# Reordering the opening of a two-layer attention decoder: the norm ahead of the modulation, sums in PSUM, four first weights instead of five

## The chip, the cores and the metric

The kernel runs on one core of a Trainium2 chip. The metric is the device time of one execution in microseconds, and the number used is the median over runs. The core has five engines with an instruction queue each, which run in order and wait for one another through semaphores: TensorE (PE, matmuls; its weight loads are listed as PEld), VectorE (DVE), ScalarE (ACT), GpSimd (POOL) and SyncE (SP), which here issues nearly all DMAs. SBUF is the working memory; PSUM is the memory that matmuls write, used here in eight banks of 128 x 512 float32.

## What is computed

Two layers of a decoder over 1024 tokens of width 1024. In each layer the input x is normalised (RMS over the width), scaled and shifted by a modulation that comes from a conditioning vector c, projected, mixed by two kinds of attention, gated, projected back and added to x. The change concerns only the start of the first layer:

```
cond  = silu(c)
mod   = cond @ w_ada[0] + b_ada[0]            # 3 x 1024: shift, scale, gate
h     = rmsnorm(x, g_pre[0]) * (1 + scale) + shift
z     = h @ ev_w_in[0]                         # the products
z_cq, z_ckv, z_kr, ... = split(z)              # first 384 columns, next 256, ...
q     = rmsnorm(z_cq, q_norm) @ w_uq           # and so on, unchanged
```

## The kernel before

Everything is kept transposed: width on the 128 partitions, tokens along the free axis, in two halves of C = 512 tokens, chunk 0 and chunk 1. So x is 2 x 8 tiles of 128 x 512, and a column block of z for one chunk is a sum over eight `kc` (128 rows of the width each). To keep float32 accuracy each h tile and each weight tile is split into a high and a low part, and each (weight block, kc) takes three matmuls (L127, L128, L130, in `kstep`): weight high by h high, weight high by h low, weight low by h high. A weight block of 128 columns thus takes 24 matmuls of 128x512 for a chunk.

The opening is written out by the string `PLAN`, whose letters the loop in `run` takes one after the other:

- `x`, `y`: issue the loads of chunk 0 or chunk 1 of x (eight DMAs of 256 KB on SP's queue).
- `r`, `s`: the norm of chunk 0 or 1. `squares` squares the eight tiles on ScalarE and adds them on VectorE (L194); `rstd` adds over partitions with a PE pass against ones (L204), computes the reciprocal square root by a chain of eleven small VectorE operations of 128 x 4 (L206 to L212), and spreads it back over 512 columns with matmuls against the identity (L216, "the transposes" below) into PSUM. `copied` moves that row block r to SBUF on ScalarE (L366).
- `A`: one of four groups of the modulation (two shift tiles and two scale tiles, so what two kc of h need). `ada` loads eight raw tiles of `w_ada`, multiplies each by its value of cond and adds them up (the first on ScalarE, L285; the other seven on VectorE, L282) into an SBUF tile `acc`; `mod_tiles` adds over partitions with a PE pass against ones (L294) and finishes the values with small VectorE operations (L303, L305).
- `W`: load a weight block, split it (high on ScalarE L91, low on GpSimd L92), and give it a PSUM bank. The blocks are the three of z_cq and the first of z_ckv, and before the change also the second.
- `n`, `m`: make the h tiles of chunk 0 or 1 that can be made (`pre_norm`): x times scale times r on VectorE (L325), plus shift on ScalarE as the high part (L331), and the low part by a subtraction on VectorE (L332). For odd kc, with `spread`, ScalarE does two operations and GpSimd does the subtraction.
- `P`: the products of all weight blocks at hand with the h tiles made since.

After the plan the opened weight blocks are evacuated, multiplied with chunk 1, and evacuated again; `keep` (L671 to L678) does this for z_cq and z_ckv and, after the last block of each, runs `rstd` for their norms. Then `project` goes on with the remaining blocks, through the same PSUM banks.

The string is the order in which the program is written. The tile library then orders each engine's instructions by priority, in which `high_priority` moves some ahead, and inserts the waits; the order shown below is that of the built program. Tiles with one tag share a fixed number of buffers (`bufs`), and a load into a buffer waits until the last reader of its former content is done. PSUM has the tags S (one tile of two banks), pt, pj and o (two banks each).

## Time and profile before

| | us |
|---|---|
| median of three runs | 1384.69 (1383.99 to 1385.03) |
| the profiled execution | 1385.66 |
| its span, first to last instruction | 1383.9 |
| its mean granted TensorE clock | 0.984 of full speed |
| TensorE busy | 1281.1 (93% of the span) |
| VectorE busy | 918.0 (66%) |
| ScalarE busy | 731.9 (53%) |
| GpSimd busy | 334.2 (24%) |

In the rows of the profile L12 is line 12 of the kernel, `out<-in` are the program's names without buffer numbers, and a row in order of time gives start and duration in us, engine, line, operation, shapes and count; the bracket behind it tells how long the engine had been idle and what released it. Matmuls are pipelined, so the distance between the starts of two of them says more than the duration of one. The span is 1.8 us shorter than the execution's time.

### The profile page before, as it was taken

The numbers are of one execution on the slowest core, as the hardware profiler recorded it, in microseconds if no ns is written. First come the engines' busy times: TensorE is split into PE (matmuls) and PEld (weight loads), VectorE is DVE, ScalarE is ACT, GpSimd is POOL, SyncE is SP. The second block draws the span as 40 slices with busy tenths as digits, with TensorE's granted clock in tenths as the row PEclk, the third lists the DMA queues.
The fourth block names the chain that finished last, engine by engine and source line by source line (L and its number), as shares of the span: only waits on it lengthen the run. The fifth ranks groups of instructions, "written<-read, shape, count | busy, mean of one in ns | idle before, by whom it ended". The sixth has DMA issues, their size and how long they took to land.

```text
span 1383.9 us, 20791 instructions
## 1 busy us (share of the span) xinstructions
PE 1281.1 (93%) x6940; PEld 1060.0 (77%) x6940; DVE 918.0 (66%) x1963; ACT 731.9 (53%) x1507; POOL 334.2 (24%) x316
## 2 busy tenths in 40 slices
PE   2798999999999999899989999999999999999996
PEld 2577788888777777777767778787888888888896
DVE  6855666777668775787977785767645464655375
ACT  4252126665557577764545544446445454556552
POOL 2242422331233215300013232221212111112400
PEclk9899999999999999999999999999999999999998
DMA  8605586556354544373633222212112121233283
GB/s 291 236 19 168 169 286 221 164 168 178 97 172 132 158 132 131 108 232 110 193 89 94 75 70 68 57 49 88 58 46 75 49 85 54 84 107 107 77 262 127
DMA packets 105132, 175.98 MB, mean 127 GB/s; under 512 B 16688, under 2 KB 25904, under 8 KB 105024
## 3 DMA queue, kind: packets, MB, share of 16 engines
q1 hardware_dynamic: 100512, 172.03, 39.4%
q10 hardware_dynamic: 4512, 2.62, 0.6%
q8 instruction: 54, 0.88, 0.3%
q14 instruction: 54, 0.44, 0.1%
HBM read 131.45 MB, written 31.74 MB: 118 GB/s over the span
## 4 chain that ended last, share of the span: by engine, by line
PE 59%; DVE 21%; issue 7%; ACT 6%; DMA 5%; POOL 1%; SPq 1%; DVEq 0%; POOLq 0%; ACTq 0%
PE pj L127 10%; PE pj L128 10%; PE pj L130 9%; PE S L441 7%; PE pt L500 4%; PE o L510 2%; DVE p L463 2%; PE S L127 2%; PE S L130 2%; PE o L509 2%; PE S L128 2%; DVE pt_l L92 2%; PE pt L216 1%; DVE acc L282 1%; DMA wr<-in_wout_dram 1%
## 5 line engine op out<-in xcount | busy, mean ns | idle before, releaser
L127 PE MATMUL pj<-h,wh 128*128 128x512 f32 (+1 forms) x816 | 340.6, 418 | 1.0 <-ACT wh L91 1.0
L128 PE MATMUL pj<-h,wh 128*128 128x512 f32 (+1 forms) x816 | 321.6, 394 | 0.0
L130 PE MATMUL pj<-h,wl 128*128 128x512 f32 (+1 forms) x800 | 314.9, 394 | 2.7 <-DVE wl L92 2.7
L92 POOL TENSOR_TENSOR wl<-wr,wh 128x512 fp32r<-128x512 f32 x126 | 164.2, 1311 | 462.7 <-ACT wh L91 424.4
L465 ACT ACTIVATE p<-p,sm 128x128 f32<-128x128 f32 (+3 forms) x192 | 148.7, 775 | 148.0 <-DVE sm L463 143.5
L92 DVE TENSOR_TENSOR pt_l<-pt,pt_h 128x512 fp32r<-128x512 f32 (+1 forms) x232 | 147.1, 635 | 107.4 <-ACT pt_h L91 105.7
L441 PE MATMUL S<-qk,qk 96*128 96x512 f32 (+5 forms) x720 | 174.6, 344 | 20.4 <-DVE sm L463 10.9
L91 ACT ACTIVATE pt_h<-pt 128x512 fp32r<-128x512 f32 (+1 forms) x232 | 127.8, 552 | 96.1 <-PE pt L500 92.5
L130 PEld LDWEIGHTS pj<-h,wl 128*128 128x128 f32 x800 | 150.5, 188 | 34.5 <-DVE wl L92 3.6
L441 PEld LDWEIGHTS S<-qk,qk 128*128 128x128 f32 (+1 forms) x720 | 120.8, 189 | 62.6 <-DVE sm L463 26.2
L127 PEld LDWEIGHTS pj<-h,wh 128*128 128x128 f32 (+1 forms) x816 | 153.6, 188 | 19.0 <-ACT wh L91 1.9
L128 PEld LDWEIGHTS pj<-h,wh 128*128 128x128 f32 (+1 forms) x816 | 154.1, 189 | 16.3 <-DVE h L92 0.2
L91 ACT ACTIVATE wh<-wr 128x512 fp32r<-128x512 f32 x165 | 101.2, 622 | 111.2 <-PE S L128 40.8
L500 PE MATMUL pt<-ident,p 128*128 128x128 f32 x840 | 134.4, 274 | 2.6 <-DVE p L944 2.6
L500 PEld LDWEIGHTS pt<-ident,p 128*128 128x128 f32 x840 | 101.2, 140 | 25.6 <-DVE p L944 4.1
L463 DVE CUSTOM_DVE_ANT_0 p<-S,mask 128x640 f32<-128x640 f32 (+7 forms) x128 | 95.9, 749 | 32.7 <-PE S L441 32.1
L509 PE MATMUL o<-pt_h,v 128*128 128x256 f32 (+1 forms) x408 | 106.5, 281 | 1.3 <-ACT pt_h L91 0.8
L510 PE MATMUL o<-pt_l,v 128*128 128x256 f32 (+1 forms) x408 | 102.3, 285 | 4.9 <-DVE pt_l L92 4.7
L347 POOL TENSOR_TENSOR t<-t,rs 128x512 f32<-128x512 f32 x26 | 36.8, 1417 | 230.8 <-DMA t<-t 208.3
L510 PEld LDWEIGHTS o<-pt_l,v 128*128 128x128 f32 x408 | 77.2, 189 | 14.8 <-DVE pt_l L92 9.6
L509 PEld LDWEIGHTS o<-pt_h,v 128*128 128x128 f32 x408 | 77.1, 189 | 9.5 <-ACT pt_h L91 3.4
L463 DVE CUSTOM_DVE_ANT_0 p<-S,x 128x128 f32<-128x128 f32 (+3 forms) x64 | 48.2, 753 | 25.0 <-PE S L445 21.8
(315 smaller groups left out, 2311.3 us busy)
## 6 DMA issues: line engine op xcount, KB each, us to landing
wr<-in_wod_dram SPq DMA_DIRECT2D x80, 256.0 KB
wr<-in_wout_dram SPq DMA_DIRECT2D x68, 256.0 KB
ad<-in_wadab_dram SPq DMA_DIRECT2D x41, 256.0 KB
wr<-in_wev_dram SPq DMA_DIRECT2D x38, 256.0 KB
raw<-in_wadaa_dram SPq DMA_DIRECT2D x32, 256.0 KB
ogd<-t SPq DMA_DIRECT2D x32, 256.0 KB
t<-t SPq DMA_DIRECT2D x106, 64.0 KB
t<-rd SPq DMA_DIRECT2D x48, 128.0 KB
```

The costliest lines, as they stand in the source:

```text
L91: nc.scalar.activation(hi, src, AF.Copy)
L92: (lo_eng or nc.vector).tensor_tensor(out=lo, in0=src, in1=hi.bitcast(F32), op=ALU.subtract)
L127: nc.tensor.matmul(p, w[0][:, k, :m], h[0], start=first, stop=False)
L128: nc.tensor.matmul(p, w[0][:, k, :m], h[1], start=False, stop=last and w[1] is None)
L130: nc.tensor.matmul(p, w[1][:, k, :m], h[0], start=False, stop=last)
L347: nc.gpsimd.tensor_tensor(out=s, in0=s, in1=self.rs[:, cs], op=ALU.mult)
L441: nc.tensor.matmul(dst, a, k[:, s], start=(n == 0), stop=(n == len(q) - 1 and not more))
L463: nc.vector.tensor_tensor_reduce(out=P[:, :n], in0=S[:, :n], in1=add, scale=-scale, scalar=init, op0=ALU.add, op1=ALU.min, accum_out=nm)
L465: nc.scalar.activation(P[:, :n], P[:, :n], AF.Exp, bias=nm, scale=-1.0, accum_out=l)
L500: nc.tensor.transpose(pt[:, n * 128:n * 128 + 128], b, self.ident)
L509: nc.tensor.matmul(o[:, qcols], w, hi[:, cols], start=start, stop=False)
L510: nc.tensor.matmul(o[:, qcols], w, lo[:, cols], start=False, stop=stop)
```

## The change

The plan is a new string. The norm of chunk 0 (`r`) comes before the first group of the modulation, each group's h tiles and products (`n`, `P`) stand ahead of the next group, the loads of chunk 1 (`y`) come after the second group, and its norm (`s`) at the end. There are four `W` instead of five, so the second block of z_ckv is done later by `project`. The sums of squares and the sums of the modulation are now kept in PSUM, in banks of the tags pt and o, until the last addition, which goes to SBUF because PE reads it. The row block r stays in PSUM (in a bank of pj for chunk 0, pt for chunk 1) and is no longer copied. The odd h tiles of chunk 0 are made like the even ones (`spread` is False). There are 12 raw buffers instead of 10. Line numbers behind `squares` shift by one.

```
--- before.py
+++ after.py
@@ -28,7 +28,7 @@
 
 
 
-PLAN = "xAWWrnWyPAWnAPWnsAPnnmmmmP"
+PLAN = "xrAWWnWPAnPyAWnPAsnPmmmmP"
 
 
 class Trunk:
@@ -185,16 +185,15 @@
     def squares(self, tiles):
 
         nc = self.nc
+        acc = self.psum("pt")
         for i, t in enumerate(tiles):
-            s = self.tmp()
+            s = self.tmp() if i else acc
             nc.scalar.activation(s, t, AF.Square)
-            if i == 0:
-                acc = s
-            else:
-                nc.vector.tensor_tensor(out=acc, in0=acc, in1=s, op=ALU.add)
-        return acc
-
-    def rstd(self, s, n, col=None):
+            if i:
+                nc.vector.tensor_tensor(out=acc if i < len(tiles) - 1 else s, in0=acc, in1=s, op=ALU.add)
+        return s
+
+    def rstd(self, s, n, col=None, home="pt"):
 
 
         nc = self.nc
@@ -211,7 +210,7 @@
             z = col if i == 2 and col is not None else y
             nc.vector.scalar_tensor_tensor(out=z, in0=w, scalar=1.5, in1=y, op0=ALU.add, op1=ALU.mult)
         y = z
-        r = self.psum("pt")[:, :nb * 128]
+        r = self.psum(home)[:, :nb * 128]
         for b in range(nb):
             nc.tensor.matmul(r[:, b * 128:b * 128 + 128], y[:, b:b + 1].to_broadcast([128, 128]), self.ident,
                              start=True, stop=True)
@@ -270,19 +269,21 @@
         nc.sync.dma_start(self.rc, I["rc"])
         nc.sync.dma_start(self.rs, I["rs"])
 
-    def ada(self, l, w, tiles, a, raw):
+    def ada(self, l, w, tiles, a, raw, part=None):
+
 
         nc = self.nc
         n = 128 * len(tiles)
         a = a[:, :n]
+        part = a if part is None else part[:, :n]
         for kc in range(8):
             r = raw()[:, :n]
             nc.sync.dma_start(r, w(kc))
             if kc:
-                nc.vector.scalar_tensor_tensor(out=a, in0=r, scalar=self.sc[:, kc:kc + 1], in1=a,
+                nc.vector.scalar_tensor_tensor(out=part if kc < 7 else a, in0=r, scalar=self.sc[:, kc:kc + 1], in1=part,
                                                op0=ALU.mult, op1=ALU.add)
             else:
-                nc.scalar.activation(a, r, AF.Copy, scale=self.sc[:, :1])
+                nc.scalar.activation(part, r, AF.Copy, scale=self.sc[:, :1])
             yield 1.0
         with self.tc.high_priority(offset=60):
             self.mod_tiles(l, tiles, a)
@@ -1171,7 +1172,7 @@
                     nc.sync.dma_start(x, I["x"][ch, :, kc])
                     xs[ch].append(x)
 
-            raw = lambda: self.t("raw", [128, C], bufs=10, pool=early)
+            raw = lambda: self.t("raw", [128, C], bufs=12, pool=early)
             ws, banks, done = [], [], []
             rs = {}
             q = 0
@@ -1181,11 +1182,11 @@
                     load_x("xy".index(step))
                 elif step in "rs":
                     ch = "rs".index(step)
-                    rs[ch] = self.copied(self.rstd(self.squares(xs[ch]), 1024))
+                    rs[ch] = self.rstd(self.squares(xs[ch]), 1024, home="pt" if ch else "pj")
                 elif step == "A":
                     tiles = [2 * q, 2 * q + 1, 8 + 2 * q, 9 + 2 * q]
                     self.drain(self.ada(0, lambda kc: I["wadaa"][q, kc], tiles,
-                                        self.t("acc", [128, C], bufs=2, pool=early), raw))
+                                        self.t("acc", [128, C], bufs=2, pool=early), raw, self.psum("o")))
                     q += 1
                 elif step == "W":
                     j = first[len(ws)]
@@ -1195,7 +1196,7 @@
                 elif step == "n":
                     with self.tc.high_priority(offset=60):
                         for kc in range(len(h[0]), min(8, 2 * q)):
-                            h[0].append(self.pre_norm(0, kc, xs[0][kc], rs[0]))
+                            h[0].append(self.pre_norm(0, kc, xs[0][kc], rs[0], False))
                 elif step == "m":
                     for kc in range(len(h[1]), min(8, len(h[1]) + 2, len(h[0]))):
                         h[1].append(self.pre_norm(0, kc, xs[1][kc], rs[1]))
```

How this moves instructions, at the three places that the prediction speaks of. The numbers at the names tell tiles apart; they differ between the two programs.

VectorE, first group of the modulation. Before (t_161 is the sum of squares of chunk 0, acc_107 the group's sum, pt_132 the PE pass over it, pt_184 the PE pass over the squares):

```order
L194 TENSOR_TENSOR t_161<-t_161,t_181 128x512
L282 SCALAR_TENSOR_TENSOR acc_107<-raw_111,sc,acc_107 128x512
L282 SCALAR_TENSOR_TENSOR acc_107<-raw_114,sc,acc_107 128x512
L282 SCALAR_TENSOR_TENSOR acc_107<-raw_117,sc,acc_107 128x512
L282 SCALAR_TENSOR_TENSOR acc_107<-raw_120,sc,acc_107 128x512
L282 SCALAR_TENSOR_TENSOR acc_107<-raw_123,sc,acc_107 128x512
L282 SCALAR_TENSOR_TENSOR acc_107<-raw_126,sc,acc_107 128x512
L282 SCALAR_TENSOR_TENSOR acc_107<-raw_129,sc,acc_107 128x512
L303 TENSOR_TENSOR mod_85<-pt_132,vecs 128x2 x2
L206 TENSOR_SCALAR sm_189<-pt_184 128x4
L305 SCALAR_TENSOR_TENSOR mod_85<-mod_85,vecs 128x2
L207 TENSOR_SCALAR sm_191<-sm_189 128x4
```

After (pt_107 is the sum of squares, pt_130 the PE pass over it, o_155 the group's sum in PSUM):

```order
L193 TENSOR_TENSOR t_127<-pt_107,t_127 128x512
L205 TENSOR_SCALAR sm_135<-pt_130 128x4
L283 SCALAR_TENSOR_TENSOR o_155<-raw_159,sc,o_155 128x512
L206 TENSOR_SCALAR sm_137<-sm_135 128x4
L283 SCALAR_TENSOR_TENSOR o_155<-raw_162,sc,o_155 128x512
L208 SCALAR_TENSOR_TENSOR sm_136<-sm_135,sm_137 128x4
L283 SCALAR_TENSOR_TENSOR o_155<-raw_165,sc,o_155 128x512
L209 TENSOR_TENSOR sm_136<-sm_136,sm_137 128x4
L283 SCALAR_TENSOR_TENSOR o_155<-raw_168,sc,o_155 128x512
L211 SCALAR_TENSOR_TENSOR sm_137<-sm_136,sm_137 128x4
```

The first small operation of the norm's chain stands ahead of the group's first sum, and the rest of the chain between the sums.

TensorE, third group. Before (pt_346 is the pass over the third group's sums, h_311 to h_317 the h tiles of the second group, the blocks of weight wx_299 and wx_384 go to o_309 and pj_394):

```order
L127 MATMUL pj_231<-h_316,wx_221 128x512
L128 MATMUL pj_231<-h_317,wx_221 128x512
L130 MATMUL pj_231<-h_316,wx_222 128x512
L128 MATMUL o_309<-h_312,wx_299 128x512
L130 MATMUL o_309<-h_311,wx_300 128x512
L127 MATMUL o_309<-h_316,wx_299 128x512
L128 MATMUL o_309<-h_317,wx_299 128x512
L294 MATMUL pt_346<-ones,acc_321 128x1 x4
L130 MATMUL o_309<-h_316,wx_300 128x512
L204 MATMUL pt_429<-ones,t_406 128x1 x4
L127 MATMUL pj_394<-h_211,wx_384 128x512
L128 MATMUL pj_394<-h_212,wx_384 128x512
```

After (pt_352 is the same pass; o_370 is the bank of the fourth weight block, h_210 to h_216 are the h tiles of the first group and h_283 to h_289 those of the second):

```order
L130 MATMUL pj_229<-h_288,wx_220 128x512
L127 MATMUL o_370<-h_210,wx_360 128x512
L128 MATMUL o_370<-h_211,wx_360 128x512
L130 MATMUL o_370<-h_210,wx_361 128x512
L127 MATMUL o_370<-h_215,wx_360 128x512
L128 MATMUL o_370<-h_216,wx_360 128x512
L130 MATMUL o_370<-h_215,wx_361 128x512
L127 MATMUL o_370<-h_283,wx_360 128x512
L128 MATMUL o_370<-h_284,wx_360 128x512
L295 MATMUL pt_352<-ones,acc_326 128x1 x4
L130 MATMUL o_370<-h_283,wx_361 128x512
L127 MATMUL o_370<-h_288,wx_360 128x512
```

The pass over the third group's sums stands now behind eight products of the fourth weight block with the tiles of the first two groups.

VectorE and TensorE at the end of chunk 0. On VectorE the square additions of chunk 1 were before among the sums of the second group (acc_266):

```order
L282 SCALAR_TENSOR_TENSOR acc_266<-raw_273,sc,acc_266 128x512
L282 SCALAR_TENSOR_TENSOR acc_266<-raw_276,sc,acc_266 128x512
L282 SCALAR_TENSOR_TENSOR acc_266<-raw_279,sc,acc_266 128x512
L282 SCALAR_TENSOR_TENSOR acc_266<-raw_282,sc,acc_266 128x512
L194 TENSOR_TENSOR t_406<-t_406,t_408 128x512
L194 TENSOR_TENSOR t_406<-t_406,t_411 128x512
L194 TENSOR_TENSOR t_406<-t_406,t_414 128x512
L194 TENSOR_TENSOR t_406<-t_406,t_417 128x512
L194 TENSOR_TENSOR t_406<-t_406,t_420 128x512
L194 TENSOR_TENSOR t_406<-t_406,t_423 128x512
L282 SCALAR_TENSOR_TENSOR acc_266<-raw_285,sc,acc_266 128x512
L194 TENSOR_TENSOR t_406<-t_406,t_426 128x512
```

After, they stand behind the fourth group's modulation (h_103 and h_105 are the last two tiles of x chunk 0, pt_451 is the sum of squares of chunk 1):

```order
L304 TENSOR_TENSOR mod_85<-pt_443,vecs 128x2 x2
L306 SCALAR_TENSOR_TENSOR mod_85<-mod_85,vecs 128x2
L193 TENSOR_TENSOR pt_451<-pt_451,t_453 128x512
L326 SCALAR_TENSOR_TENSOR h_103<-h_103,mod_85,pj_149 128x512
L326 SCALAR_TENSOR_TENSOR h_105<-h_105,mod_85,pj_149 128x512
L193 TENSOR_TENSOR pt_451<-pt_451,t_456 128x512
L333 SCALAR_TENSOR_TENSOR h_500<-h_103,mod_85,h_499 128x512
L193 TENSOR_TENSOR pt_451<-pt_451,t_459 128x512
L333 SCALAR_TENSOR_TENSOR h_505<-h_105,mod_85,h_504 128x512
L193 TENSOR_TENSOR pt_451<-pt_451,t_462 128x512
L193 TENSOR_TENSOR pt_451<-pt_451,t_465 128x512
L193 TENSOR_TENSOR pt_451<-pt_451,t_468 128x512
```

On TensorE the pass over the squares of chunk 1 (pt_429) and the transposes of its r (pt_448) stood before among the products of the third group's tiles:

```order
L127 MATMUL o_309<-h_401,wx_299 128x512
L128 MATMUL o_309<-h_402,wx_299 128x512
L130 MATMUL o_309<-h_401,wx_300 128x512
L216 MATMUL pt_448<-ident,sm_436 128x128
L294 MATMUL pt_480<-ones,acc_455 128x1 x4
L216 MATMUL pt_448<-ident,sm_436 128x128 x3
L127 MATMUL pj_394<-h_396,wx_384 128x512
L128 MATMUL pj_394<-h_397,wx_384 128x512
L130 MATMUL pj_394<-h_396,wx_385 128x512
L127 MATMUL pj_394<-h_401,wx_384 128x512
```

After (pt_474 is the pass over the squares, pt_493 takes the transposes, h_533 is the first h tile of chunk 1):

```order
L130 MATMUL o_370<-h_499,wx_361 128x512
L127 MATMUL o_370<-h_504,wx_360 128x512
L203 MATMUL pt_474<-ones,t_471 128x1 x4
L128 MATMUL o_370<-h_505,wx_360 128x512
L130 MATMUL o_370<-h_504,wx_361 128x512
L215 MATMUL pt_493<-ident,sm_481 128x128 x4
L203 MATMUL pt_731<-ones,t_582 128x1 x4
L127 MATMUL pj_606<-h_533,wh_188 128x512
L127 MATMUL S_637<-h_533,wh_199 128x512
L127 MATMUL pj_700<-h_533,wx_360 128x512
```

The transposes and the pass behind them are now the last things between the products of chunk 0 and those of chunk 1.

More of the change, by code (lines that the diff above doesn't have):

```diff
@@ L26 @@
 SC96 = 96 ** -0.5
-PLAN = "xAWWrnWyPAWnAPWnsAPnnmmmmP"
+PLAN = "xrAWWnWPAnPyAWnPAsnPmmmmP"
 class Trunk:
@@ L187, in squares, with rstd @@
         nc = self.nc
+        acc = self.psum("pt")
         for i, t in enumerate(tiles):
-            s = self.tmp()
+            s = self.tmp() if i else acc
             nc.scalar.activation(s, t, AF.Square)
-            if i == 0:
-                acc = s
-            else:
-                nc.vector.tensor_tensor(out=acc, in0=acc, in1=s, op=ALU.add)
-        return acc
-    def rstd(self, s, n, col=None):
+            if i:
+                nc.vector.tensor_tensor(out=acc if i < len(tiles) - 1 else s, in0=acc, in1=s, op=ALU.add)
+        return s
+    def rstd(self, s, n, col=None, home="pt"):
         nc = self.nc
@@ L213, in rstd @@
         y = z
[L214 removed]
+        r = self.psum(home)[:, :nb * 128]
         for b in range(nb):
@@ L271, in setup2, with ada @@
         nc.sync.dma_start(self.rs, I["rs"])
-    def ada(self, l, w, tiles, a, raw):
+    def ada(self, l, w, tiles, a, raw, part=None):
         nc = self.nc
@@ L277, in ada @@
         a = a[:, :n]
+        part = a if part is None else part[:, :n]
         for kc in range(8):
@@ L281, in ada @@
             if kc:
-                nc.vector.scalar_tensor_tensor(out=a, in0=r, scalar=self.sc[:, kc:kc + 1], in1=a,
+                nc.vector.scalar_tensor_tensor(out=part if kc < 7 else a, in0=r, scalar=self.sc[:, kc:kc + 1], in1=part,
                                                op0=ALU.mult, op1=ALU.add)
             else:
-                nc.scalar.activation(a, r, AF.Copy, scale=self.sc[:, :1])
+                nc.scalar.activation(part, r, AF.Copy, scale=self.sc[:, :1])
             yield 1.0
@@ L1172, in load_x @@
                     xs[ch].append(x)
-            raw = lambda: self.t("raw", [128, C], bufs=10, pool=early)
+            raw = lambda: self.t("raw", [128, C], bufs=12, pool=early)
             ws, banks, done = [], [], []
@@ L1183, in run @@
                     ch = "rs".index(step)
-                    rs[ch] = self.copied(self.rstd(self.squares(xs[ch]), 1024))
+                    rs[ch] = self.rstd(self.squares(xs[ch]), 1024, home="pt" if ch else "pj")
                 elif step == "A":
@@ L1187, in run @@
                     self.drain(self.ada(0, lambda kc: I["wadaa"][q, kc], tiles,
-                                        self.t("acc", [128, C], bufs=2, pool=early), raw))
+                                        self.t("acc", [128, C], bufs=2, pool=early), raw, self.psum("o")))
                     q += 1
```

3 lines of the change are left out of this document (1 added, 2 removed).

## Prediction

> **What bounds the kernel now.** I read the page's first part, then a table of four stretches, then each engine's instructions in order of time from 0 to 140 us. The table's columns are busy time and instruction count for PE, PEld, DVE, ACT and POOL, then granted clock, DMA share and GB/s.
>
> ```profile
> span 1383.9 us, 20791 instructions
> PE 1281.1 (93%) x6940; PEld 1060.0 (77%) x6940; DVE 918.0 (66%) x1963; ACT 731.9 (53%) x1507; POOL 334.2 (24%) x316
> ...
> 0.00:80.60 80.60, 47.38 (x184) 36.61 (x185) 60.51 (x104) 33.65 (x55) 23.74 (x20) 0.92 0.65 226
> 80.60:110.00 29.40, 28.56 (x122) 22.25 (x121) 9.89 (x13) 14.30 (x26) 15.70 (x12) 1.00 0.11 32
> 110.00:140.00 30.00, 25.30 (x133) 21.45 (x132) 18.50 (x61) 8.07 (x15) 7.04 (x6) 0.89 0.58 192
> 140.00:1383.90 1243.90, 1179.84 (x6507) 979.67 (x6506) 829.06 (x1786) 675.86 (x1412) 287.76 (x279) 0.99 0.39 121
> ```
>
> TensorE is the bound overall, so the change is worth what it saves or adds in PE idle time and half-rate time. Before 80.6 us PE is busy 47 of 81 us while VectorE is busy 61: there VectorE feeds PE. From 80.6 to 110 PE is full. The DMA share (0.65) is no bound in the opening. "Product" below means one 128x512 matmul; "sums" means the eight scaled rows of a group added up, and the PE pass with ones behind them.
>
> First group, in order of time (start us, us, engine):
>
> ```profile
> 9.08 3.88 DVE L194 TENSOR_TENSOR t<-t,t 128x512 f32<-128x512 f32 x5 [1.33 <-ACT t L190]
> ...
> 12.87 5.47 DVE L282 SCALAR_TENSOR_TENSOR acc<-raw,sc,acc 128x512 f32<-128x512 f32 x7
> ...
> 18.40 1.87 PE L294 MATMUL pt<-ones,acc 128*128 128x1 f32 x8 [18.40 <-DVE acc L282]
> ...
> 22.01 0.16 DVE L206 TENSOR_SCALAR sm<-pt 128x4 f32<-128x4 f32 x1 [1.48 <-PE pt L204]
> ...
> 24.24 2.05 PE L216 MATMUL pt<-ident,sm 128*128 128x128 f32 x8 [2.27 <-issue]
> ...
> 26.33 0.60 ACT L366 ACTIVATE t<-pt 128x512 f32<-128x512 f32 x1 [6.38 <-PE pt L216]
> ...
> 28.62 0.79 PE L127 MATMUL S<-h,wh 128*128 128x512 f32 x1 [2.33 <-ACT h L331]
> ```
>
> The sums end at 18.34, the norm's chain of eleven small operations takes 22.01 to 24.24, and the first product starts at 28.62. Groups two to four, and chunk 1:
>
> ```profile
> 28.80 1.72 POOL L92 TENSOR_TENSOR wx<-wr,wx 128x512 fp32r<-128x512 f32 x1
> 29.31 1.76 DVE L332 SCALAR_TENSOR_TENSOR h<-h,mod,h 128x512 fp32r<-128x512 f32 x1
> ...
> 30.99 5.03 DVE L282 SCALAR_TENSOR_TENSOR acc<-raw,sc,acc 128x512 f32<-128x512 f32 x4
> ...
> 44.43 1.84 PE L294 MATMUL pt<-ones,acc 128*128 128x1 f32 x8 [5.28 <-DVE acc L282]
> ...
> 46.76 1.42 DVE L325 SCALAR_TENSOR_TENSOR h<-h,mod,t 128x512 f32<-128x512 f32 x2
> ...
> 47.54 0.72 ACT L331 ACTIVATE h<-h,mod 128x512 fp32r<-128x512 f32 x1 [7.81 <-DVE h L325]
> ...
> 48.40 0.71 PE L127 MATMUL S<-h,wh 128*128 128x512 f32 x1
> ...
> 58.17 1.00 PE L204 MATMUL pt<-ones,t 128*128 128x1 f32 x8
> ...
> 62.71 0.40 PE L127 MATMUL S<-h,wh 128*128 128x512 f32 x1
> ...
> 72.23 0.50 PE L127 MATMUL S<-h,wh 128*128 128x512 f32 x1
> ...
> 80.68 0.40 PE L127 MATMUL o<-h,wx 128*128 128x512 f32 x1
> ```
>
> PE reaches the second, third and fourth pair of h tiles at 48.40, 62.71 and 72.23. The norm of chunk 1 (58.17) is over long before PE needs it, so PE crosses to chunk 1 at 80.68 without a stop, 120 products done. From 46.27 (end of the PE pass) to the next VectorE step is 0.49, from there to the product 1.64: 2.13 for each group.
>
> Prices, from single instructions:
>
> ```profile
> 63.42 0.39 PE L127 MATMUL pj<-h,wx 128*128 128x512 f32 x1
> ...
> 68.75 0.40 PE L130 MATMUL o<-h,wx 128*128 128x512 f32 x1
> ...
> 64.89 0.75 DVE L282 SCALAR_TENSOR_TENSOR acc<-raw,sc,acc 128x512 f32<-128x512 f32 x1
> ...
> 65.68 0.75 DVE L282 SCALAR_TENSOR_TENSOR acc<-raw,sc,acc 128x512 f32<-128x512 f32 x1
> ...
> 85.06 1.74 POOL L678 TENSOR_TENSOR t<-t,t 128x512 f32<-128x512 f32 x1
> ...
> 85.58 0.74 DVE L673 SCALAR_TENSOR_TENSOR qk<-S,vecs,qk 128x512 fp32r<-128x512 f32 x1
> ...
> 92.65 1.29 POOL L92 TENSOR_TENSOR wl<-wr,wh 128x512 fp32r<-128x512 f32 x1 [2.08 <-ACT wh L91]
> ```
>
> From 63.42 to 68.75 are 23 steps: 0.232 a product at the full clock. A VectorE sum comes every 0.785. VectorE with both tensors in SBUF waits while POOL works (1.76 at 29.31, about 1.26 each at 30.99); with one of them in PSUM it took 0.74 under a POOL instruction of 1.74.
>
> **The change, part by part.** Times are of the profiled execution. No row has ScalarE writing PSUM or VectorE summing in PSUM in place; the bounds are 0.60 and 0.72 (ACT at 26.33, 47.54) and 0.74 and 0.75 (DVE at 85.58, 64.89), so at most 0.1 a group either way, and I take the present period.
>
> *Norm first, no copy of it.* VectorE's queue now has the chain's first operation ahead of the sums, and it waits for PE: squares end 12.96, PE 1.87, sums start 14.95 instead of 12.87 and end 7 x 0.785 later, 20.45 (2.1 late). PE sums to 22.4, modulation and last chain step to 22.95, transposes 2.05, and without the copy (0.60) the multiply starts at 25.1; first product 25.1 + 1.64 = 26.7 (1.9 early).
>
> *Second group.* Its seven sums no longer stand behind those of x chunk 1 (now eight loads and eight squares later). Two multiplies, one sum, then two subtractions with both inputs in SBUF, beside three POOL splits of 1.29: 0.75 to 1.75 each, so the remaining six sums (4.7) end between 34.6 and 36.0; I take 35.3. PE pass 1.0 to 1.84, so 36.7; product at 38.8 (9.6 early). The odd h tiles lose ScalarE and POOL work (spread off): one VectorE subtraction more for each, counted above and below at 0.75.
>
> *Third group.* "Products ahead of the next group" makes VectorE wait for each PE pass before it goes on. Multiplies 37.2 to 38.65, then sum, subtraction, sum, subtraction (0.75 each and 0.55 behind a POOL split) to 42.2, five sums to 46.1. But the PE pass over them stands behind 18 products that need the tile of 42.2: 4.2 us at full clock, 7.7 at half; I take 6.0, so 48.2, pass to 49.2: VectorE waits 3 us for PE's order. Product at 51.3 (11.4 early).
>
> *Fourth group.* The first scaled row is ScalarE's and stands behind two squares, an h tile and a weight split (0.60 to 0.72 each): 51.2 + 3.3 = 54.5. Seven sums to 60.0, PE pass to 61.4, one square addition ahead of the multiply, product at 64.2 (8.0 early).
>
> *The switch to chunk 1.* Its square additions, before done at leisure, now come last on VectorE: ten operations of 0.72 from 62.6, to 69.8. PE's own products end between 69.6 and 72.2; the pass for the norm is over at 72.4; the chain (2.2), two evacuations of 0.66 in between and part of a POOL addition take 4.0: 76.4. Transposes 0.9 to 2.05 (1.5): 77.9, product at 79.5, bounds 76.0 and 82.5. For about 6 us PE has nothing but small passes.
>
> *Four weights.* At 79.5 PE has done 96 products, not 120. Chunk 1 takes 96 x 0.232 = 22.3, and 1.2 to 2.5 for tiles that come one pair in 2 us and for a clock still at half (1.9): 103.7. The 48 products left for later cost 11.1: 114.8. More raw buffers and the moved loads I cost at nothing: up to the last load of the fourth group SP issues 56 of 262 KB, at 226/0.65 = 348 GB/s 42 us, and that group is wanted at 54.5. If that cover went, the squares of chunk 1, which stand on ScalarE ahead of the third group's h tile, would hold that tile up.
>
> What those 114.8 stand against, and what follows:
>
> ```profile
> 110.09 0.94 PE L204 MATMUL pt<-ones,t 128*128 128x1 f32 x8
> ...
> 111.08 0.16 DVE L206 TENSOR_SCALAR sm<-pt 128x4 f32<-128x4 f32 x1 [4.34 <-PE pt L204]
> ...
> 112.28 3.20 POOL L92 TENSOR_TENSOR p<-wr,p 128x512 fp32r<-128x512 f32 x3
> ...
> 113.62 1.19 DVE L210 TENSOR_TENSOR sm<-sm,sm 128x4 f32<-128x4 f32 x1
> ...
> 117.36 2.05 PE L216 MATMUL pt<-ident,sm 128*128 128x128 f32 x8 [3.43 <-DVE sm L212]
> 119.20 1.71 PE L204 MATMUL pt<-ones,t 128*128 128x1 f32 x8
> ...
> 121.76 0.63 PE L130 MATMUL S<-h,wl 128*128 128x512 f32 x1
> ...
> 123.47 0.55 PE L127 MATMUL S<-h,wh 128*128 128x512 f32 x1
> ...
> 138.13 1.13 PE L216 MATMUL pt<-ident,rkc 128*128 128x128 f32 x8 [1.15 <-DVE rkc L212]
> ```
>
> Before, 240 products are done at 110.09: the change is then 4.7 behind. Next the old kernel waits 3.43 for a chain whose small operations POOL holds up, and pays 1.7 on two passes and seven products x 0.2 at half rate (from 121.76 to 123.47 one came in 0.43): 6.5. The changed one has the same chain under 14 products instead of 12: I work out 3.0 of wait and 0 to 3.1 at half rate (1.6): 1.9 given back. The 1.15 at 138.13 is mostly covered by five more products: 0.9 back. Sum: 4.7 - 1.9 - 0.9 = 1.9 us slower. The profiled execution took 1385.66 (span 1383.9 and 1.8 around it), 1.0 above the median 1384.69, so 1387.6 in its terms and 1386.6 as a median: 0.14%, inside the 0.2% (2.8 us) that a measurement here can tell.
>
> One rule speaks for the change. VectorE at 85.58, with one tensor in PSUM, did not wait for POOL. The Trainium skill, page "SBUF — State Buffer", section "Who interferes with whom", says that VectorE shares a read port with GpSimd and contends only with two SBUF inputs; the trace agrees (0.74 against 1.76). By it the sums cost 0.785 whatever POOL does, as above; without it the second group's would cost about 2 us more.
>
> **The rivals.** *Faster: PE stays at full clock and the switch is short.* All lower ends: chunk 1 at 76.0, 76.0 + 22.3 + 1.2 + 11.1 = 110.6, so 0.5 behind, then 3.5 and 0.9 back: 3.9 faster, 1380.8. For it: the first gap between groups shrinks from 19.8 us (28.62 to 48.40) to 12. Against: each group still waits for a PE pass and 2.13 behind it.
>
> *Slower: PE is at half rate through the opening.* At 121.76 a wait of 3.43 was enough to halve the rate for three us. The new order has such a wait before each group and a longer one at the switch. Upper ends there: 82.5 + 22.3 + 2.5 + 11.1 = 118.4, 8.3 behind, 2.8 back: 5.5 slower, 1390.2. It decides once the product of the fourth group starts after about 65.5. The Trainium skill, page "TensorE: Matmul & The Clock Gate", section "Part 1: The HAM clock gate", says that an idle window of some 3.4 us halves the clock and a busy one restores it; the trace agrees at 117.36, and by that rule the switch restarts PE at half rate.
>
> *The sums in PSUM wait for POOL after all*, or cost more in place: about two operations x 0.95 = 1.9 more, 1388.5. Against it the row at 85.58.
>
> **How the numbers follow.** Forecast 0.42, faster rival 0.25, half clock 0.25, PSUM 0.08. The forecast's own spread (1384 to 1389) gives 0.03 faster, 0.26 within 0.2%, 0.13 slower; the first rival 0.21 and 0.04 within; the second 0.03 within and 0.22 slower; the third 0.04 and 0.04. Together 0.24, 0.37, 0.39. The range runs from just below the faster rival, 1380.0, to a little past the half clock, 1391.5.
>
> **What would show it.** First product near 26.7; second, third, fourth group near 38.8, 51.3, 64.2; the third PE pass waits for PE's own products, not for VectorE; a PE gap of some 5 us ending on the chain of chunk 1's norm, chunk 1 near 79.5; then 96 products. If chunk 1 starts before 77, or the wait near 105 is gone, the time is lower than I say; if sums under POOL last over 1 us, the PSUM step is wrong.

## The result, and the profile after

The changed kernel takes 1403.53 us (median of four, 1401.45 to 1406.48), the kernel before, run beside it, 1384.34: a ratio of 1.0127, interval 1.0108 to 1.0146. It is 19 us slower, far outside the forecast of 1386.6 (1380.0 to 1391.5).

The first two lines of the page of after:

```profile
span 1401.2 us, 20813 instructions
PE 1292.3 (92%) x6940; PEld 1066.9 (76%) x6940; DVE 912.1 (65%) x1967; ACT 728.5 (52%) x1501; POOL 323.4 (23%) x312
```

A table of stretches for after (busy time and count of PE, PEld, DVE, ACT and POOL, then granted clock, DMA share, GB/s):

```profile
110.00:140.00 30.00, 25.08 (x116) 20.44 (x116) 15.18 (x49) 7.03 (x14) 7.73 (x7) 0.89 0.53 173
140.00:180.00 40.00, 39.34 (x180) 31.93 (x180) 26.65 (x34) 9.59 (x18) 20.84 (x16) 1.00 0.60 183
180.00:230.00 50.00, 44.45 (x191) 34.78 (x191) 29.39 (x49) 14.36 (x30) 11.41 (x13) 0.97 0.80 257
310.00:1310.00 1000.00, 953.80 (x5183) 783.15 (x5182) 656.60 (x1454) 566.45 (x1186) 230.21 (x226) 0.99 0.33 103
```

The same for before:

```profile
140.00:180.00 40.00, 36.91 (x168) 29.87 (x168) 27.55 (x35) 8.72 (x16) 18.86 (x14) 1.00 0.62 191
180.00:230.00 50.00, 49.89 (x237) 40.02 (x236) 32.19 (x60) 21.46 (x45) 10.00 (x12) 1.00 0.78 256
310.00:1310.00 1000.00, 953.70 (x5188) 784.95 (x5189) 659.83 (x1452) 564.17 (x1179) 229.94 (x224) 0.99 0.34 103
```

From 180 to 230 TensorE, full before, is idle 5.6 of 50 us. The middle of the program (310 to 1310) is the same. Where the 17.3 us of span come from is seen by matching the same instruction in both traces and taking the difference of the starts (median over the matched instructions of VectorE, ScalarE, GpSimd and SyncE in the stretch of 10 us, from 300 on of 50, that begins at the time named, a time of before; a plus is later than before). In the stretches up to 230 the matched instructions themselves differ by a few us, so these entries are good to 1 or 2 us. The kernels below the first row are those of the experiments, in the profiled run of each:

| | 140 | 170 | 200 | 230 | 300 | 850 | 1350 |
|---|---|---|---|---|---|---|---|
| after | +5.1 | +4.2 | +10.5 | +12.5 | +13.9 | +13.9 | +16.5 |
| before, four weights | +1.9 | +4.7 | +11.6 | +16.9 | +18.0 | +17.3 | +19.2 |
| before, background early | -1.6 | -1.1 | +8.2 | +9.6 | +11.5 | +14.9 | +15.5 |
| before, banks shifted | -0.5 | +0.8 | +4.2 | +6.7 | +9.0 | +9.7 | +9.8 |
| after, five weights | 0.0 | -2.3 | -0.3 | +0.5 | +2.6 | +1.2 | +1.2 |
| after, banks back | +1.0 | -0.6 | +9.2 | +10.0 | +10.3 | +8.5 | +8.7 |
| after, banks and background back | +0.2 | +0.9 | +3.8 | +3.9 | +6.6 | +5.5 | +5.8 |
| after, five weights, s early | -5.2 | -4.8 | -4.1 | -4.5 | -4.2 | -6.4 | -6.4 |

So after the opening the changed kernel is about 5 behind, not 19; some 10 of the 17 us are lost between 170 and 300, where the prediction costed nothing. The 3.5 us that after loses behind 1310 are not there in the two kernels of the table with the banks put back, and were not pursued.

The opening in order of time, after (first to fourth group, the switch to chunk 1, its end):

```profile
15.02 0.75 DVE L283 SCALAR_TENSOR_TENSOR o<-raw,sc,o 128x512 f32<-128x512 f32 x1
18.44 3.72 POOL L92 TENSOR_TENSOR wl<-wr,wh 128x512 fp32r<-128x512 f32 x3 [18.00 <-DMA wr<-in_wev_dram]
18.85 0.88 DVE L208 SCALAR_TENSOR_TENSOR sm<-sm,sm 128x4 f32<-128x4 f32 x1
20.87 0.73 DVE L283 SCALAR_TENSOR_TENSOR acc<-raw,sc,o 128x512 f32<-128x512 f32 x1
27.79 0.79 PE L127 MATMUL S<-h,wh 128*128 128x512 f32 x1 [1.59 <-ACT h L332]
30.05 2.96 POOL L92 TENSOR_TENSOR wx<-wr,wx 128x512 fp32r<-128x512 f32 x2
30.57 3.91 DVE L283 SCALAR_TENSOR_TENSOR o<-raw,sc,o 128x512 f32<-128x512 f32 x5
39.23 0.79 PE L127 MATMUL S<-h,wh 128*128 128x512 f32 x1 [2.05 <-ACT h L332]
48.37 0.95 PE L295 MATMUL pt<-ones,acc 128*128 128x1 f32 x8
49.35 0.23 DVE L304 TENSOR_TENSOR mod<-pt,vecs 128x2 f32<-128x2 f32 x2 [3.26 <-PE pt L295]
51.36 0.50 PE L127 MATMUL S<-h,wh 128*128 128x512 f32 x1 [1.00 <-ACT h L332]
63.29 0.80 PE L127 MATMUL S<-h,wh 128*128 128x512 f32 x1 [2.52 <-ACT h L332]
77.36 2.07 PE L215 MATMUL pt<-ident,sm 128*128 128x128 f32 x8 [4.63 <-DVE sm L211]
81.03 0.79 PE L127 MATMUL pj<-h,wh 128*128 128x512 f32 x1
105.73 1.05 PE L215 MATMUL pt<-ident,sm 128*128 128x128 f32 x8
```

And the place of the largest single stop of TensorE behind the opening, after: VectorE's background sums (`ad`, the groups of the modulation that run beside the later products), and TensorE's pass over them:

```profile
188.11 1.54 DVE L283 SCALAR_TENSOR_TENSOR ad<-ad,sc 128x512 f32<-128x512 f32 x2 [3.10 <-DMA ad<-in_wadab_dram]
190.90 0.75 DVE L283 SCALAR_TENSOR_TENSOR ad<-ad,sc 128x512 f32<-128x512 f32 x1 [1.25 <-DMA ad<-in_wadab_dram]
191.79 0.35 PE L295 MATMUL pt<-ones,ad 128*128 128x1 f32 x2 [4.28 <-DVE ad L283]
```

The ten us around it, with the columns of the table above:

```profile
185.00:195.00 10.00, 5.72 (x22) 4.46 (x21) 2.87 (x5) 1.27 (x2) 1.71 (x2) 0.86 0.97 314
```

VectorE waits for loads in a stretch in which the DMA engines are busy 0.97 of the time, TensorE waits for VectorE, and the clock falls to 0.86.

### The profile page after: what moved, and what is told of

Read it like the earlier page. It is cut to its first block, busy times and chain, and to the rows that moved or that the text cites. A ratio compares the mean times of both kernels' runs of the same rounds, so it can differ in the third digit from the quotient of the medians.

```text
span 1401.2 us, 20813 instructions
## 1 busy us (share of the span) xinstructions
PE 1292.3 (92%) x6940; PEld 1066.9 (76%) x6940; DVE 912.1 (65%) x1967; ACT 728.5 (52%) x1501; POOL 323.4 (23%) x312
## 4 chain that ended last, share of the span: by engine, by line
PE 40%; DVE 12%; issue 5%; ACT 5%; DMA 3%; SPq 1%; POOL 0%; DVEq 0%; POOLq 0%; ACTq 0%
PE pj L127 8%; PE pj L128 7%; PE pj L130 7%; PE S L442 5%; PE pt L501 3%; DVE p L464 2%; PE o L511 2%; PE o L510 1%; DVE pt_l L92 1%; PE S L127 1%; PE S L130 1%; PE S L128 1%; DMA wr<-in_wout_dram 1%; DMA t<-t 1%; DVE t L347 1%
## 5 line engine op out<-in xcount | busy, mean ns | idle before, releaser
L127 PE MATMUL pj<-h,wh 128*128 128x512 f32 (+2 forms) x824 | 345.5, 420 | 1.6 <-ACT wh L91 1.2
L128 PE MATMUL pj<-h,wh 128*128 128x512 f32 (+2 forms) x824 | 326.0, 396 | 0.0
L442 PE MATMUL S<-qk,qk 96*128 96x512 f32 (+5 forms) x720 | 175.1, 345 | 21.6 <-DVE sm L464 11.1
L127 PEld LDWEIGHTS pj<-h,wh 128*128 128x128 f32 (+1 forms) x824 | 156.1, 190 | 20.4 <-ACT wh L91 2.3
L128 PEld LDWEIGHTS pj<-h,wh 128*128 128x128 f32 (+1 forms) x824 | 156.1, 189 | 17.7 <-POOL h L92 0.5
L91 ACT ACTIVATE wh<-wr 128x512 fp32r<-128x512 f32 (+1 forms) x164 | 99.8, 621 | 96.0 <-PE pj L128 35.9
L511 PEld LDWEIGHTS o<-pt_l,v 128*128 128x128 f32 x408 | 77.2, 189 | 13.9 <-DVE pt_l L92 8.5
```

Source lines behind the costliest of these rows:

```text
L91: nc.scalar.activation(hi, src, AF.Copy)
L127: nc.tensor.matmul(p, w[0][:, k, :m], h[0], start=first, stop=False)
L128: nc.tensor.matmul(p, w[0][:, k, :m], h[1], start=False, stop=last and w[1] is None)
L442: nc.tensor.matmul(dst, a, k[:, s], start=(n == 0), stop=(n == len(q) - 1 and not more))
L511: nc.tensor.matmul(o[:, qcols], w, lo[:, cols], start=False, stop=stop)
```

## The experiments

In the diffs `+` is what the experiment has. "The dense stage" is the call of `project` behind the opening: the rest of the blocks on five PSUM banks in rotation, with the background groups put between (0.3 of a load for each kc step), up to the attention at some 210 to 220 us.

**Four weights alone, the place of the background, the place of s.**

Four weights in the old plan:

```diff
-PLAN = "xAWWrnWyPAWnAPWnsAPnnmmmmP"
+PLAN = "xAWWrnWyPAWnAPnsAPnnmmmmP"
```

> The kernel before with one W less in its plan (four first weights), nothing else changed. Theory A (the loss behind the opening comes from the number of first weights: one more block in the dense stage puts each background group of the modulation 16 steps earlier in TensorE's order, where its loads have not landed): the opening gets shorter by about 11 us of products that are done later, TensorE waits 3 to 5 us for the fourth background group near 180 to 195 us, and the time is 6 to 11 us above before, 1391 to 1396. Theory B (the loss is the opening's order, whose delay of some 5 us moves later stages against the DMA queues): the time is within 2 us of before, and there is no wait of over 2 us for the background sums.

1403.42 us, ratio 1.0135 (1.0090 to 1.0180): the whole loss, with the old opening. Its trace has the same stop as after, `ad` at the background pass, and a second one at the start of the attention:

```profile
191.75 0.56 PE L294 MATMUL pt<-ones,ad 128*128 128x1 f32 x2 [3.77 <-DVE ad L282]
229.20 0.69 PE L500 MATMUL pt<-ident,p 128*128 128x128 f32 x2 [3.42 <-ACT p L465]
```

The order of the opening is not needed for the loss.

The background 16 steps later in the changed kernel, and 16 steps earlier in the kernel before (`both` starts its counter at the last argument; without it, at 0):

```diff
-        self.drain(self.both(self.project(first[K:], dense=True, deep=1), behind, 0.3))
+        self.drain(self.both(self.project(first[K:], dense=True, deep=1), behind, 0.3, -4.8))
```

> The changed kernel, with the background modulation started 16 steps later in the dense stage (its counter starts at -4.8 instead of 0, so that it stands where it stood before against the blocks that follow). The opening and the four weights are unchanged. Theory A: the wait of 4.28 us at 191.79 is gone, and with it the half clock behind it; 6 to 10 us below after, 1393 to 1397. Theory B: no change, 1401 to 1405.

> The kernel before, with the background modulation 16 steps earlier in the dense stage (its counter starts at 4.8). Five weights and the old opening. Theory A: a wait of 2 to 5 us for the background sums appears near 180 to 195 us and the time is 4 to 9 us above before, 1388 to 1393. Theory B: within 2 us of before. If theory A holds for this one and not for the one with four weights in the old plan, it is the place of the background alone; if the other way round, it is the extra block itself (its weight load, its bank).

Later in after: 1407.18, ratio 1.0163 (1.0136 to 1.0189), nothing regained, so theory A failed there in the time. Its sign did come, the wait of 4.28 is gone; but VectorE now stands at a late load a little earlier, and TensorE waits behind it for the bank S, which VectorE frees at 193.38:

```profile
189.96 0.75 DVE L283 SCALAR_TENSOR_TENSOR ad<-ad,sc 128x512 f32<-128x512 f32 x1 [3.96 <-DMA ad<-in_wadab_dram]
194.11 0.50 PE L127 MATMUL S<-qk,wh 128*128 128x512 f32 x1 [3.26 <-DVE t L720]
```

Earlier in before (4.8 in place of -4.8): 1401.13, ratio 1.0108 (1.0085 to 1.0131), 16 us lost by this edit alone, more than expected. The trace of this run shows how, VectorE and then TensorE:

```profile
198.03 3.25 DVE L282 SCALAR_TENSOR_TENSOR ad<-ad,sc 128x512 f32<-128x512 f32 x2 [4.79 <-DMA ad<-in_wadab_dram]
203.06 0.67 DVE L719 TENSOR_TENSOR t<-S,g 128x512 f32<-128x512 f32 x1
203.79 0.80 PE L127 MATMUL S<-qk,p 128*128 128x512 f32 x1 [5.58 <-DVE t L719]
```

VectorE's queue stands 4.79 us at a background sum whose load is late; the evacuation of S stands behind it, and TensorE cannot write S. A background sum that nothing urgent needs holds up what is urgent, because the two stand in one engine's queue in this order. In the kernel before, the place of the background can thus cost 16 us; in after, moving it back gave nothing, so there had to be a second cause.

The norm of chunk 1 ahead of the fourth group:

```diff
-PLAN = "xrAWWnWPAnPyAWnPAsnPmmmmP"
+PLAN = "xrAWWnWPAnPyAWnPsAnPmmmmP"
```

> The changed kernel with the norm of chunk 1 (s) ahead of the fourth group instead of behind it. Theory 1 (the switch to chunk 1 waits for the chain of that norm, as predicted): the wait of 4.63 us before the transposes at 77.36 goes, the fourth group's product comes some 5 us later than 63.3 because seven square additions of 0.78 now stand ahead of its sums, and the first product of chunk 1 comes at 76 to 79 instead of 81.0: 2 to 5 us below after, 1398 to 1401. Rival (VectorE's total work bounds the opening, wherever the norm stands): chunk 1 still starts at 80.5 to 82, within 2 us of after.

1398.38 (1395.44 to 1403.99), 5 us below after and where theory 1 had it, though the interval of its ratio, 1.0065 to 1.0129, overlaps that of after; the profiled run is the slowest of the four. There chunk 1 starts at 76.06 instead of 81.03, the wait of 4.63 is gone from the switch (one of 3.95 for the same chain stands at 64.68, inside chunk 0), and the kernel is 4.7 ahead of after at 140 us (+0.4 against +5.1).

**Buffers, fewer background groups, five weights.**

```diff
-                ready.append(load(jobs[k], ("p", "p") if deep and k % 2 else None))
+                ready.append(load(jobs[k], ("p", "p") if deep and k % 2 == 0 else None))
```

> The changed kernel; in the dense stage the weight blocks of even instead of odd number go to the buffers of tag p. With four first weights the count of blocks starts one earlier, so the change had swapped which later block lies in p and which in wh; this swaps it back, and the last block before the attention lies in wh again, as before. Theory P (the swapped buffers make the loss: the last block's weights sit in p when the attention wants p, and the loads behind wait on SP's queue): 6 to 10 us below after, 1393 to 1397, the wait for p near 226 us gone. Theory D (the stretch from 175 to 215 us is limited by the DMA queues and any shift of it costs, whatever buffers are used): within 3 us of after, 1400 to 1406.

> The changed kernel with the weight buffers swapped back and the background modulation 16 steps later: behind its first block the dense stage is then the same program as before, block for block, and only starts about 5 us later. Theory P or a place theory: 1388 to 1393, the 5 us of the opening and little else. Theory D: a wait of over 2 us still falls between 175 and 215 us, because SP's loads and stores meet the same DMA limit at another phase: 1396 to 1406.

1405.22 (ratio 1.0128, 1.0107 to 1.0148), and with the background 16 steps later as well 1406.64 (1.0129, 1.0091 to 1.0168): with the banks as the change has them, the weight buffers are not it.

```diff
-        self.drain(self.both(self.project(first[K:], dense=True, deep=1), behind, 0.3))
+        self.drain(self.both(self.project(first[K:], dense=True, deep=1), islice(behind, 24), 0.3))
```

> The changed kernel with the background modulation stopped in the dense stage after 24 loads, three groups; the other five groups follow in the attention stage. Theory D (the eight loads of 256 KB of the fourth group, each waiting for one of three buffers on SP's queue, beside the stores of q, k and v): the waits of 4.28 us at 191.79 and the half clock behind it go, DMA share between 185 and 210 us falls from about 0.87 to 0.6 to 0.7, 6 to 10 us below after, 1393 to 1397. Theory P: within 3 us of after.

1396.34, ratio 1.0070 (1.0052 to 1.0088): 7 us regained, the wait of 4.28 gone, and TensorE full from 185 to 210 us. The lag stays at 5 to 6 us until 210 and then grows to 12 at the start of the attention.

Five weights, in the new opening:

```diff
-PLAN = "xrAWWnWPAnPyAWnPAsnPmmmmP"
+PLAN = "xrAWWnWPAnPyAWnPAWsnPmmmmP"
...
-                    rs[ch] = self.rstd(self.squares(xs[ch]), 1024, home="pt" if ch else "pj")
+                    r = self.rstd(self.squares(xs[ch]), 1024)
+                    rs[ch] = r if ch else self.copied(r)
```

> The changed kernel with the fifth first weight back (its load behind the fourth group's), the row block r of chunk 0 copied to SBUF by ScalarE, since the fifth block needs its bank; the order of norm, modulation and products and the sums in PSUM stay as changed. If the four weights alone carry the loss, as the run of the old plan with four weights suggests: 1383 to 1390, no wait of over 2 us between 175 and 215 us. If the new opening carries it too: 1396 or more.

1387.03, ratio 1.0003 (0.9992 to 1.0015). All of the change but the number of weights (and the copy of r that the fifth bank asks for) costs nothing.

**Six weights, five with s early, two controls.**

Six weights in the old plan; to make room for the sixth, `wx` gets 8 buffers instead of 6 and `raw` 8 instead of 10:

```diff
-PLAN = "xAWWrnWyPAWnAPWnsAPnnmmmmP"
+PLAN = "xAWWrnWyPAWnAPWnsAPWnnmmmmP"
```

> The kernel before with six first weights (one W more ahead of the last two h steps; the room for it comes from raw, 8 buffers instead of 10). Theory F (each first weight block gives TensorE 24 products to do in time in which the opening's VectorE work leaves it idle, 24 x 0.232 = 5.6 us, and takes its load out of the dense stage; four weights lost that, six should gain it): 3 to 8 us below before, 1377 to 1382. Rival (before sits at the best point, since five blocks already fill the idle time ahead of chunk 1, where TensorE crosses to chunk 1 without a stop): the sixth block's chunk 0 products only push chunk 1 back by what they take, within 3 us of before or slower.

1402.81, ratio 1.0115 (1.0093 to 1.0138). Theory F failed; the rival allowed for a slower kernel, but the sixth block's products, which it names, are 5.6 us and not 16. That six lose as four do led to the banks, below.

Five weights in the new opening, s early:

```diff
-PLAN = "xrAWWnWPAnPyAWnPAWsnPmmmmP"
+PLAN = "xrAWWnWPAnPyAWnPsAWnPmmmmP"
```

> Five weights in the new opening, as in the run before it, and the norm of chunk 1 ahead of the fourth group instead of behind it. In the four-weight kernel that move gave 5.1 us. If it takes away the wait of 3.04 us ahead of the transposes at 79.19 here too: 2 to 4 us below the five-weight run, 1383 to 1385. Rival: with five weights TensorE has products of chunk 0 to fill that time and the fourth group comes 5 us later, so no gain: 1386 to 1389.

1380.64, ratio 0.9957 (0.9939 to 0.9975), faster than both kernels and 6 us below five weights with a late s, more than the 2 to 4 expected. The stretch from 58 to 84 us in after, and below it in the kernel with five weights and a late s:

```profile
58.00:84.00 26.00, 17.01 (x63) 13.81 (x64) 19.73 (x39) 9.55 (x16) 3.85 (x3) 0.72 0.00 0
58.00:84.00 26.00, 20.06 (x92) 16.21 (x90) 21.69 (x40) 10.02 (x18) 6.14 (x5) 0.90 0.09 31
```

The same in this kernel:

```profile
58.00:84.00 26.00, 23.25 (x109) 17.89 (x108) 21.47 (x44) 14.22 (x24) 10.52 (x9) 1.00 0.11 31
```

And its transposes of chunk 1's norm, in order of time:

```profile
65.66 0.49 PE L215 MATMUL pt<-ident,sm 128*128 128x128 f32 x2 [0.58 <-DVE sm L211]
```

The chain of the norm runs between the sums of the fourth group, and its wait is 0.58 instead of 3.04 with the late s (4.63 in after, with four weights); TensorE crosses to chunk 1 at full clock (1.00 against 0.90, and 0.72 in after).

The kernel before with `islice(behind, 24)`:

> The kernel before with the background modulation stopped in the dense stage after three groups, the control for the same edit of the changed kernel, which gave 7 us. Theory D (only a kernel whose background sums TensorE waits for gains): before has no such wait, so within 3 us of before, 1383 to 1388, or a little slower since the other groups fall into the attention stage. Rival (the fourth group's loads cost every kernel in the DMA-bound stretch): 3 to 6 us below before, 1379 to 1382.

1388.22, ratio 1.0012 (0.9997 to 1.0027): theory D. Before has no wait there, so fewer groups gain it nothing.

And after with three groups, with the first v later:

```diff
-        Vn = self.load_v(0)
+        with self.tc.high_priority(offset=-80):
+            Vn = self.load_v(0)
```

> The changed kernel with three background groups in the dense stage, as in the run before it, and the first load and split of v later in the order, so that on ScalarE the split stands behind the first four probability tiles as in the kernel before, not ahead of them. Theory O (at the start of the attention the order on ScalarE, a split that waits 2.17 us for its load from DRAM ahead of what TensorE needs, costs the 6 us lost between 210 and 240 us): the wait of 1.83 us at 225.70 and the half clock behind it go, 2 to 5 us below the run before it, 1391 to 1394. Rival (the attention's start is late for other reasons, loads of q and k among them): within 2 us, 1394 to 1398.

1395.56, ratio 1.0058 (1.0035 to 1.0082), beside 1396.34 without it: in the times inconclusive, its runs spread over 8.6 us. In the trace the lag at 230 is +4.3 instead of +10.2 and the wait at 225.70 is gone, but 4 us are lost again by 850. So the wait hung on that order; what it is worth in the end is not shown.

**The banks.** `project` begins its rotation anew. Five blocks for two chunks are ten banks, two full turns, so a new start changes nothing; with four the blocks behind get other banks, and S, one tile of two banks, goes to others of them. The last block before the attention shows it: the last product of the dense stage and TensorE's first step of the attention, before (the product goes to o):

```profile
209.50 0.39 PE L130 MATMUL o<-qk,wl 128*128 128x512 f32 x1
209.73 0.45 PE L441 MATMUL S<-qk,qk 96*128 96x128 f32 x3
```

After (it goes to S, which the attention needs next):

```profile
219.93 0.39 PE L130 MATMUL S<-qk,p 128*128 128x512 f32 x1
...
221.20 0.52 PE L442 MATMUL S<-qk,qk 96*128 96x128 f32 x3
```

This meeting is no stop by itself: after, four products of the next block fill the time in between. What the banks are worth, the next runs show. `project` gets an argument `turn`, -1 unless named; in the call of the dense stage it is 2 in after, which gives each later block the bank that it had before, and 1 in before, which shifts them as the change does:

```diff
-        self.turn_of = -1
+        self.turn_of = turn
```

> The changed kernel; the rotation of PSUM banks in the dense stage goes on from where the opening left it instead of from the start, so that each later block has the bank that it had before. Theory R (the rotation: S is one tile of two banks, and a block that has it waits until both halves are read; with four weights other, slower blocks get it, and the last block ahead of the attention too): the waits on S and the loss behind 175 us go, the 5 us of the opening stay, 8 to 12 us below after, 1390 to 1395. Theory D (DMA and background loads in that stretch, whatever the banks): within 3 us of after, 1400 to 1406.

1395.35, ratio 1.0079 (1.0053 to 1.0105): 8 us regained. Up to 170 us nothing is left of the loss (-0.6). Then VectorE and TensorE, the same picture as in the old kernel with an early background:

```profile
198.64 1.54 DVE L283 SCALAR_TENSOR_TENSOR ad<-ad,sc 128x512 f32<-128x512 f32 x2 [4.35 <-DMA ad<-in_wadab_dram]
...
201.96 0.68 DVE L720 TENSOR_TENSOR t<-S,g 128x512 f32<-128x512 f32 x1
...
202.69 0.80 PE L127 MATMUL S<-qk,wh 128*128 128x512 f32 x1 [3.32 <-DVE t L720]
```

> The kernel before, five weights and the old opening, with the rotation two banks on in the dense stage, so that each block there has the bank that it has in the changed kernel. Theory R: 5 to 12 us above before, 1391 to 1398, lost between 175 and 310 us. Theory D: within 2 us of before, 1384 to 1388.

1398.21, ratio 1.0090 (1.0064 to 1.0116): with five weights and the old opening the banks alone cost 11 us. The largest waits between 140 and 300 us, all before a write to S:

```profile
167.56 0.50 PE L127 MATMUL S<-qk,p 128*128 128x512 f32 x1 [1.50 <-DVE t L701]
174.27 0.50 PE L140 MATMUL S<-wh,qk 128*128 128x512 f32 x1 [1.18 <-DVE t L701]
179.21 0.50 PE L140 MATMUL S<-wh,qk 128*128 128x512 f32 x1 [2.33 <-ACT t L725]
222.94 1.25 PE L441 MATMUL S<-qk,qk 96*128 96x512 f32 x6 [1.16 <-DVE sm L463]
```

The kernel before has two of this kind in the same stretch:

```profile
161.10 0.50 PE L127 MATMUL S<-qk,p 128*128 128x512 f32 x1 [1.66 <-DVE t L356]
172.77 0.50 PE L140 MATMUL S<-wh,qk 128*128 128x512 f32 x1 [1.43 <-ACT t L725]
```

So the four waits are 3 us more than these two; the rest of the 11 us is not assigned to single waits.

> The kernel before with six first weights, and the rotation in the dense stage set so that each later block has the bank that it had with five. Theory R: the loss against five weights shrinks from 16 us to 4 or less, or turns into a gain of up to 5: 1379 to 1391. Theory D: 1399 to 1405, as without it.

1402.68, ratio 1.0121 (1.0093 to 1.0150): not the banks alone. Its trace has the stop that the early background made in the kernel before, a late load on VectorE and TensorE waiting for S:

```profile
197.50 1.54 DVE L282 SCALAR_TENSOR_TENSOR ad<-ad,sc 128x512 f32<-128x512 f32 x2 [5.39 <-DMA ad<-in_wadab_dram]
200.89 0.80 PE L127 MATMUL S<-qk,wh 128*128 128x512 f32 x1 [3.70 <-DVE t L719]
```

With six weights the background stands 16 steps later against the blocks. It was not tried to put that back, nor to give `raw` its buffers again; why six lose stays open.

> The changed kernel with four weights, the norm of chunk 1 ahead of the fourth group, and the rotation as in the first run of this call. Theory R: both gains add, 5 us of the switch and 8 to 12 of the banks, 1384 to 1390. Theory D: 1396 to 1401, as with the earlier norm alone.

1395.39, ratio 1.0059 (1.0035 to 1.0084): 3 us below the earlier norm alone with overlapping intervals, no better than the banks alone; the two gains did not add. A wait of 4.59 for S behind the background sums stands at 200.96, where the banks alone have 3.32.

**Banks and background together** (`turn=2` and -4.8).

> The changed kernel, four weights, with both the bank rotation and the place of the background modulation as they were against the blocks that follow. If these two are the whole loss behind the opening: 1384 to 1389, within 3 us of before, no wait of over 2.5 us between 175 and 210 us. If a third cause is left (the extra block's load and evacuations in the dense stage, the swapped weight buffers): 1391 to 1396, as with the banks alone.

> The same with the norm of chunk 1 ahead of the fourth group. If the gain of the earlier norm (3 to 5 us in the four-weight kernels, 6 in the five-weight kernel) adds to the first run of this call: 1379 to 1384, as fast as the five-weight kernel with the earlier norm (1380.6), which the number of weights then no longer matters for. If it is lost again behind the opening: within 2 us of the first run of this call.

1391.79, ratio 1.0038 (1.0024 to 1.0051), and with the earlier norm 1389.39, ratio 1.0019 (1.0010 to 1.0028). The wait at 202.69 is gone. Some 5 us of the loss are left, gathered between 170 and 300 us (the lag goes from 0.9 to 6.6) with no wait of TensorE over 1 us from 175 on, and the earlier norm gives 2 us, not 5. The expectation named a third cause for such a rest: the fifth block's load and evacuations in the dense stage, or the swapped weight buffers. Neither was tried with banks and background put back. The four combinations of the changed kernel, medians:

| | background early | background as before |
|---|---|---|
| banks as the change has them | 1403.5 | 1407.2 |
| banks as before | 1395.4 | 1391.8 |

The background's place pays only once the banks are as before: 3.6 us then, with the intervals (1.0053 to 1.0105 and 1.0024 to 1.0051) just apart. That is why moving it alone showed nothing.

## Why the prediction was wrong

**Norm first.** Right in kind, the first product at 27.79 for 26.7 and 28.62 before. The sums began as said (15.02), but three of the chain's small operations between them, with both inputs in SBUF, are stretched while GpSimd works from 18.44 to 22.16 (0.88 at 18.85 for one that takes 0.15 at 16.48), and the last sum starts at 20.87, where the prediction had the sums end at 20.45.

**Second to fourth group.** 39.23, 51.36 and 63.29 for 38.8, 51.3 and 64.2. The third pass stood behind TensorE's own products as said: VectorE waited 3.26 for it (said 3).

**Sums in PSUM.** Right: 3.91 for five at 30.57, 0.78 each (said 0.785), beside GpSimd's 2.96 at 30.05. The Trainium skill, page "SBUF — State Buffer", section "Who interferes with whom", says that a VectorE instruction with at most one SBUF input, outside the 2-port modes, does not contend with GpSimd; the trace agrees (0.78 in these rows).

**The switch.** 81.03 for 79.5, wait 4.63 for the chain, 0.72 of the clock from 58 to 84: inside its bounds. The earlier norm took the wait away from the switch: worth 6 us with five weights, about 5 with four (intervals overlapping), but 0 and 2 in the two kernels with the banks put back.

**Four weights: the step that failed.** "The 48 products left for later cost 11.1" counted them as time on TensorE and nothing else. Chunk 1 ended as reckoned, 105.73 for 103.7. But leaving the fifth block to the dense stage changes that stage too: its banks, since the rotation begins anew, and the background's place, since that counts kc steps from the stage's start. The stretch from 140 us on, nine tenths of the program, had no term in the sum, and the text gave no reason for that. In its place the runs show 16 us for the number of weights alone (1403.53 against 1387.03 with five in the same opening, 18.7 in the old one). They put the banks at 8 us (after) and 11 (before), the background's place at 16 in the old kernel and 3.6 in after once the banks are as before; the two interact, and some 5 of 17 to 19 us stay unassigned. The forecast said slower and the kernel is slower, but by a loss that the sum did not contain: that the directions agree is luck.

**What was to be given back.** The wait near 117 came as reckoned (2.71 at 113.61 for 3.0), and the 1.15 near 138 is covered as said. New are two waits of the passes over the second norm's sums, whose last block is now in the dense stage:

```profile
113.61 2.01 PE L215 MATMUL pt<-ident,sm 128*128 128x128 f32 x8 [2.71 <-DVE t L258]
120.74 1.05 PE L203 MATMUL pt<-ones,t 128*128 128x1 f32 x8 [0.70 <-POOL t L679]
132.81 1.05 PE L203 MATMUL pt<-ones,t 128*128 128x1 f32 x8 [1.51 <-POOL t L679]
```

With the banks put back only the first is left, and the lag at 140 is +1.0 (banks) and +0.2 (banks and background), where the sum said +1.9. So the opening by itself was sized to within 2 us; in after it came out at 5 because the fifth block, the first of the dense stage, already met other banks.

**The rivals.** Half clock came in part (0.72 from 58 to 84 us, where before has 0.93; 0.89 from 110 to 140, as before), but its own sign, a fourth group later than 65.5, did not (63.29), and five weights with the same order, at 0.90 from 58 to 84, lose nothing. All the rivals lay in the opening, none behind it, and the range took only the opening's bounds; that is why it did not hold the time.

## What to carry to other kernels

When a change moves a block of work from one stage to the next, go through everything in the next stage that counts from its start: bank rotations, buffer parities, work woven in at a rate. Try the bank rotation going on where it was rather than anew (8 us here with four weights), and keep sums that wait for late loads, and that nothing urgent needs, from standing in VectorE's queue ahead of evacuations (16 us in the old kernel). A reordering is best tried one part at a time: here the new opening with an earlier norm and five weights is 6 us faster than before, hidden under the 16 that one letter of the plan cost.
